# Query and key transposes taken before the high/low split, with ScalarE row sums and earlier weight splits

## The chip, the cores and the metric

The kernel runs on one core of one Trainium2 chip. The metric is the device time of one launch in microseconds (us); lower is better. Four engines compute: TensorE (PE in the profile, with its weight loads as PEld), VectorE (DVE), ScalarE (ACT) and GpSimd (POOL). SyncE (SP) issues the DMAs.

## The reference

One encoder layer on a sequence of 1024 tokens of width 1024, in float32:

```python
x = LN0(alpha*x + 0.5*SwiGLU_1(x))
u = x @ W_in                    # -> q | k | v | z | x_ssd | B | C | dt
q = rope(rms(q) * q_norm)       # 8 query heads of 64
k = rope(rms(k) * k_norm)       # 2 key/value heads of 64
a = softmax(q @ k.T / 8) @ v    # every 4 query heads share one key/value head
s = bidirectional chunked SSD scan of conv(x_ssd, B, C), gated by SiLU(z)
x = LN1(alpha*x + concat(a, s) @ W_out)
x = LN2(alpha*x + 0.5*SwiGLU_2(x))
x = LN3(alpha*x + sigmoid(x @ W_g + b_g) * (p @ W_p))
```

`rms` divides a head's 64 values by the root of their mean square. `rope` turns pairs of values by an angle that depends on the token.

## The kernel before

Matrix products run on a rounded float32 type (`F32R`). To keep the precision, most factors are split in two: the rounded value ("hi") and the rest ("lo", the plain value less hi). `mm3` (L116) forms a product from three matmuls for each block of 128: hi with lo, lo with hi, hi with hi. A split is one ScalarE copy (L108) and one VectorE subtraction (the helper `lo`, L87).

The part that matters here is `qkv_part` (L841). It comes between the last tiles of z (`z_part`) and the products that feed the convolution (`xbc_gemm`, L967).

- **q stage.** For each of 8 tiles of 128 tokens, `qq` (L832) multiplies the tile with the q weights: 24 matmuls of 512 columns into one buffer of the PSUM pool `sm`, which has four.
- **kv stage.** For each of the same 8 tiles, `kv` (L820) does it with the weights of k, v and dt: 24 matmuls of 272 columns into an `sm` buffer.
- **Behind each product**, `norm` (L862) squares the heads on ScalarE (L865), sums the squares on VectorE (L867), scales them (L868) and takes the power -0.5 on GpSimd (L870). `rope` (L873) refines that power (`newton`, L125), multiplies the values by it (L877, the last reader of the product's `sm` buffer) and turns them (L883 to L885) into the tile `qn`.
- **The split before the transpose.** `q_back` (L917) copies `qn` to the hi half of a tile `qs` on ScalarE (L920); the lo half is a VectorE subtraction, done one step later through the list `los`. So one head is 128 values wide, hi beside lo. `turn` transposes each of the 8 heads on TensorE (L926) into a buffer of the pool `big` (two buffers), and one ScalarE copy (L927) writes `Q`, with hi in 64 partitions and lo in the other 64. `kv_back` (L899) does the same for k: each of the two heads is written twice side by side, its hi half and its lo half are transposed apart (4 transposes, L909, into an `sm` buffer), and one copy (L910) writes `K`.
- **v** is split straight from the product (L895, L896), and dt is added to its bias (L892).

`step` (L933) sets the order: for tile t it issues the transposes of an earlier tile, then `norm` of t, then the outstanding `lo`, then `rope` of tile t-1. The transposes of a q tile stand behind the product three tiles later. What is left of k is put into `pend`, and `xbc_gemm` issues it between its halves.

The order on TensorE is the program's (`in_order`). The other engines' orders, and the buffers, are set by a planner that goes by its own estimates; `behind(engine)` makes what follows queue behind the last instruction written for that engine.

Weights come in by DMA from the SP queue into one of two `raw` buffers, and are split from there into a `blk` buffer of the pool `ring`, which has ten. In the q stage the eight blocks of q weights hold eight of them. `kv_weights` (L812) loads and splits the eight blocks for k, v and dt at tiles 6 and 7 of q, so six of them need a buffer that a q block leaves. `xbc_weights` (L961) loads and splits two blocks for each of the eight groups of convolution channels where the group's product is written.

Of the kernel before, what the change touches and what calls it, by code (L numbers as in the profile page):

```python
# [9 lines left out]
F32 = mybir.dt.float32  # L10
F32R = mybir.dt.float32r
BF16 = mybir.dt.bfloat16
AF = mybir.ActivationFunctionType
ALU = mybir.AluOpType
# [22 lines left out]
class Layer:  # L37
# [773 lines left out]

    def kv_weights(self, part):  # L812
        if part == 0:
            self.wkv = []
        for k in ((0,), (3, 6))[part]:
            n = min(3, KD - k)
            r = self.raw(self.I["wkv"][:, k * 272:(k + n) * 272], n * 272)
            self.wkv += [self.split(r[:, i * 272:(i + 1) * 272], 272) for i in range(n)]

# [21 lines left out]
    def qkv_part(self, c, xT):  # L841
        nc, tc, I = self.nc, self.tc, self.I
        Q, K, V = self.qkv
        tabs = c.enter_context(tc.tile_pool(name="tabs", bufs=1))
        wk = c.enter_context(tc.tile_pool(name="qwork", bufs=2))
        cs = tabs.tile([P, NT, HD], F32, name="cs")
        sn = tabs.tile([P, NT, HD], F32, name="sn")
# [14 lines left out]
        def norm(ps, nh):  # L862
            v = ps.rearrange("p (h d) -> p h d", d=HD)
            sq = wk.tile([P, nh, HD], F32, name="sq")
            nc.scalar.activation(out=sq, in_=v, func=AF.Square)  # L865
            ss = self.small.tile([P, 16], F32, name="ss")[:, :nh]
            nc.vector.reduce_sum(ss, sq, axis=AX.X)  # L867
            nc.vector.tensor_scalar(out=ss, in0=ss, scalar1=1.0 / HD, scalar2=RMS_EPS, op0=ALU.mult, op1=ALU.add)  # L868
            r = self.small.tile([P, 16], F32, name="qr")[:, :nh]
            nc.gpsimd.tensor_tensor(out=r, in0=ss, in1=self.mhalf[:, :nh], op=ALU.pow)  # L870
            return v, nh, sq, ss, r

        def rope(v, nh, m, ss, r, nm, t):  # L873

            self.newton(r, ss, nh)
            qn = wk.tile([P, nh, HD], F32, name="qn")
            nc.vector.tensor_tensor(out=qn, in0=v, in1=r.unsqueeze(2).broadcast_to([P, nh, HD]), op=ALU.mult)  # L877
            T1, T2 = (x[:, t] for x in T[nm])
            H2 = HD // 2
            for a in range(2):  # L880
                o = slice(a * H2, (a + 1) * H2)
                i = slice((1 - a) * H2, (2 - a) * H2)
                nc.vector.tensor_tensor(out=m[:, :, o], in0=qn[:, :, i], in1=T2[:, o].unsqueeze(1).broadcast_to([P, nh, H2]), op=ALU.mult)  # L883
            nc.vector.tensor_tensor(out=qn, in0=qn, in1=T1.unsqueeze(1).broadcast_to([P, nh, HD]), op=ALU.mult)
            nc.vector.tensor_tensor(out=qn, in0=qn, in1=m, op=ALU.add)  # L885
            return qn

# [11 lines left out]
        def kv_back(t, st):  # L899

            kn = rope(*st, "k", t).unsqueeze(2).broadcast_to([P, NKV, 2, HD])
            kd = wk.tile([P, NKV, 2, 2, HD], F32R, name="qs", bufs=4)
            nc.scalar.copy(out=kd[:, :, 0], in_=kn)

            def turn():
                pt = self.pss().rearrange("p (g j t) -> p g j t", g=NKV, j=2)
                for g in range(NKV):
                    for j in range(2):
                        nc.tensor.transpose(out=pt[:, g, j], in_=kd[:, g, j].rearrange("p a d -> p (a d)").bitcast(F32), identity=self.ident)  # L909
                nc.scalar.copy(out=K[:, :, :, t * P:(t + 1) * P], in_=pt)  # L910
            late.append(turn)
            return kd[:, :, 1], kn, kd[:, :, 0]

# [3 lines left out]
        def q_back(t, st):  # L917
            qs = wk.tile([P, NQ, 2, HD], F32R, name="qs", bufs=4)
            qn = rope(*st, "q", t)
            nc.scalar.copy(out=qs[:, :, 0], in_=qn)  # L920

            def turn():
                pt = self.psb().rearrange("p (h t) -> p h t", t=P)
                qv = qs.bitcast(F32)
                for hh in range(NQ):
                    nc.tensor.transpose(out=pt[:, hh], in_=qv[:, hh].rearrange("p a d -> p (a d)"), identity=self.ident)  # L926
                nc.scalar.copy(out=Q[:, :, t * P:(t + 1) * P], in_=pt)  # L927
            late.append(turn)
            return qs[:, :, 1], qn, qs[:, :, 0]

        backs, los = [], []

        def step(t, ps, front, back, keep=1):  # L933
# [5 lines left out]
            if los:  # L939
                self.lo(*los.pop())  # L940
            if backs:
                los.append(backs.pop()())
            if front:
                backs.append(lambda: back(t, st))

        tables("q", HD ** -0.5)
        for t in range(NT):
            ps = self.qq(t, xT)
            if t >= NT - 2:
                self.kv_weights(t - NT + 2)  # L950
            step(t, ps, q_front, q_back)
        for t in range(NT):
            ps = self.kv(t, xT)
            step(t, ps, kv_front, kv_back, 2)
            if t == 0:
                tables("k", 1.0)
        self.pend += [lambda: step(NT, None, None, None)] * 4
        self.x0 = self.xbc_gemm(0, xT, 1)
        assert not late and not backs and not los

    def xbc_weights(self, j):  # L961
        return [b.rearrange("p l (k c) -> p l k c", c=P) for b in self.wload(self.I["wx"][j])]

# [1056 lines left out]
```

## Time and profile before

| | |
|---|---|
| time, median of 3 runs | 1940.51 us (1940.17 to 1941.06) |
| profiled execution | 1940.12 us |
| its span, first to last instruction | 1938.3 us |
| PE busy | 1927.8 us (99%) |
| DVE busy | 1523.9 us (79%) |
| ACT busy | 881.6 us (45%) |
| POOL busy | 417.2 us (22%) |
| granted TensorE clock | 0.999 |

The span and all busy times are of the profiled execution; 1.8 us of its time lie outside the span. In rows of the profile, L12 is line 12 of the kernel, `out<-in` names the tiles written and read (buffer numbers left out), `x8` is a count, and `<-` in brackets names what ended an engine's idle time. Instructions of one engine overlap a little, so a start-to-start distance is the better measure of what one costs. In this profile the q stage's first product begins at about 696 us, the kv stage's at 744.35 us and the first convolution product at 772.90 us.

### The profile page before, as it was taken

The numbers are of one execution on the slowest core, as the hardware profiler recorded it, in microseconds if no ns is written. First come the engines' busy times: TensorE is split into PE (matmuls) and PEld (weight loads), VectorE is DVE, ScalarE is ACT, GpSimd is POOL, SyncE is SP. The second block draws the span as 40 slices with busy tenths as digits, with TensorE's granted clock in tenths as the row PEclk, the third lists the DMA queues.
The fourth block names the chain that finished last, engine by engine and source line by source line (L and its number), as shares of the span: only waits on it lengthen the run. The fifth ranks groups of instructions, "written<-read, shape, count | busy, mean of one in ns | idle before, by whom it ended". The sixth has DMA issues, their size and how long they took to land.

```text
span 1938.3 us, 25689 instructions
## 1 busy us (share of the span) xinstructions
PE 1927.8 (99%) x9146; PEld 1607.8 (83%) x9146; DVE 1523.9 (79%) x2362; ACT 881.6 (45%) x1510; POOL 417.2 (22%) x308
## 2 busy tenths in 40 slices
PE   9999999999999999999999999999999999999998
PEld 7888888888888889888888888888888888888886
DVE  8977777767678668758998888997787786877698
ACT  7433333334444224538897877633333333444311
POOL 0144544430001032001131001014444540001011
PEclk9999999999999999999999999999999999999999
DMA  8334544549866111241002663253544539976022
GB/s 315 127 130 153 194 181 147 195 163 389 280 220 210 63 43 48 86 123 67 6 1 85 219 215 122 93 176 138 190 175 168 183 122 359 331 263 223 28 78 97
DMA packets 147714, 310.34 MB, mean 160 GB/s; under 512 B 18129, under 2 KB 30801, under 8 KB 147585
## 3 DMA queue, kind: packets, MB, share of 16 engines
q1 hardware_dynamic: 147584, 308.69, 45.6%
q8 instruction: 72, 1.18, 0.2%
q14 instruction: 58, 0.47, 0.1%
HBM read 217.21 MB, written 91.42 MB: 159 GB/s over the span
## 4 chain that ended last, share of the span: by engine, by line
PE 99%; DVE 0%; DMA 0%; ACT 0%; DVEq 0%; issue 0%; SPq 0%
PE sm L122 56%; PE big L519 12%; PE sm L519 9%; PE big L122 6%; PE big L1189 3%; PE sm L1211 3%; PE sm L1226 2%; PE sm L1227 1%; PE sm L639 1%; PE sm L1407 1%; PE sm L1306 1%; PE sm L1317 1%; PE big L1722 0%; PE big L926 0%; PE big L224 0%; PE sm L224 0%
## 5 line engine op out<-in xcount | busy, mean ns | idle before, releaser
L122 PE MATMUL sm<-xh,blk 128*128 128x512 f32 x1424 | 439.8, 389 | 0.0
L122 PEld LDWEIGHTS sm<-xh,blk 128*128 128x128 f32 x1424 | 267.3, 188 | 55.4
L122 PE MATMUL sm<-xl,blk 128*128 128x512 f32 x736 | 283.8, 389 | 0.0
L122 PE MATMUL sm<-blk,xl 128*128 128x512 f32 (+2 forms) x704 | 208.1, 369 | 0.0
L108 ACT CAST blk<-raw 128x512 fp32r<-128x512 f32 (+1 forms) x168 | 101.1, 611 | 214.8 <-PE sm L122 133.2
L87 DVE TENSOR_TENSOR blk<-raw,blk 128x512 fp32r<-128x512 f32 (+1 forms) x168 | 142.5, 852 | 53.8 <-ACT blk L108 53.2
L108 ACT CAST blk<-s 128x512 fp32r<-128x512 f32 x172 | 105.7, 622 | 153.3 <-PE sm L122 125.7
L87 DVE TENSOR_TENSOR blk<-s,blk 128x512 fp32r<-128x512 f32 x176 | 142.3, 812 | 39.6 <-ACT blk L108 36.8
L178 POOL TENSOR_TENSOR ln_k<-ln_k,mhalf 128x1 f32<-128x1 f32 x32 | 37.7, 1183 | 578.4 <-DVE ln_k L177 562.2
L122 PEld LDWEIGHTS sm<-xl,blk 128*128 128x128 f32 x736 | 138.2, 188 | 28.7
L122 PE MATMUL sm<-blk,xh 128*128 128x512 f32 (+2 forms) x448 | 158.0, 373 | 0.0
L122 PEld LDWEIGHTS sm<-blk,xl 128*128 128x128 f32 x704 | 127.8, 188 | 20.6
L267 POOL TENSOR_TENSOR s<-raw 128x512 f32<-128x512 f32 x34 | 57.8, 1699 | 381.9 <-DVE blk L87 370.6
L519 PE MATMUL big<-xh 128*128 128x512 f32 x576 | 138.8, 390 | 0.0
L87 DVE TENSOR_TENSOR xh<-blk,xh 128x1024 fp32r<-128x1024 f32 x78 | 95.3, 1222 | 52.1 <-ACT xh L465 46.1
L465 ACT CAST xh<-blk 128x1024 fp32r<-128x1024 f32 x78 | 82.2, 1054 | 109.0 <-PE big L519 47.1
L465 ACT CAST xl<-blk 128x1024 fp32r<-128x1024 f32 x76 | 80.2, 1055 | 112.9 <-PE sm L519 43.1
L87 DVE TENSOR_TENSOR xl<-blk,xl 128x1024 fp32r<-128x1024 f32 x76 | 92.9, 1222 | 43.1 <-ACT xl L465 40.8
L519 PEld LDWEIGHTS big<-xh 128*128 128x128 f32 x576 | 107.8, 188 | 22.2
L519 PE MATMUL big<-xl 128*128 128x512 f32 x480 | 115.8, 390 | 0.0
L122 PE MATMUL sm<-xET2h,blk 128*128 128x512 f32 x352 | 108.4, 389 | 0.0
L122 PE MATMUL sm<-xET3h,blk 128*128 128x512 f32 x352 | 108.3, 389 | 0.0
(357 smaller groups left out, 4118.6 us busy)
## 6 DMA issues: line engine op xcount, KB each, us to landing
raw<-in_wi_dram SPq DMA_DIRECT2D x81, 512.0 KB
blk<-hS SPq DMA_DIRECT2D x154, 256.0 KB
hS<-h SPq DMA_DIRECT2D x88, 256.0 KB
wr<-in_wo_dram SPq DMA_DIRECT2D x44, 512.0 KB
blk<-wT SPq DMA_DIRECT2D x88, 256.0 KB
hS<-sg SPq DMA_DIRECT2D x66, 256.0 KB
wT<-wr SPq DMA_DIRECT2D x66, 256.0 KB
blk<-in_wo_dram SPq DMA_DIRECT2D x66, 256.0 KB
```

The lines of the kernel that those rows point to most:

```text
L87: (eng or self.nc.vector).tensor_tensor(out=out, in0=full, in1=hi.bitcast(F32), op=ALU.subtract)
L108: self.nc.scalar.copy(out=b[:, 0, :n], in_=src)
L122: self.nc.tensor.matmul(ps, lhsT=a, rhs=b, start=(i == 0), stop=(i == n - 1))
L178: nc.gpsimd.tensor_tensor(out=r, in0=v, in1=self.mhalf[:, :1], op=ALU.pow)
L267: lambda: G.tensor_tensor(out=s1, in0=a21, in1=a22, op=ALU.add),
L465: A.copy(out=b[:, :, 0], in_=r)
L519: nc.tensor.matmul(ps[q], lhsT=b[:, 0, x, cut], rhs=b[:, 1, y], start=j == i == 0, stop=j == NP - 1 and i == 2)
L639: nc.tensor.matmul(o, lhsT=pT[t // 4][k][:, i, c], rhs=we[n][k][:, j], start=k + i + j == 0, stop=k + i == 2)
L1189: nc.tensor.matmul(ps[:, n * 512:(n + 1) * 512], lhsT=Q[:, h, q0:q0 + P], rhs=K[:, h // 4, j, n * 512:(n + 1) * 512], start=j == 0, stop=j ...
L1211: nc.tensor.transpose(out=pt[:, k], in_=pr[:, kk * P:(kk + 1) * P], identity=self.ident)
L1226: nc.tensor.matmul(po, lhsT=vw, rhs=pth[k // 4][:, k % 4], start=k == 0, stop=False)
L1227: nc.tensor.matmul(po, lhsT=vw, rhs=ptl[k // 4][:, k % 4], start=False, stop=k == KD - 1)
```

## The change

Four things change in `qkv_part` and what it calls.

1. **Transposes of plain values.** For q, `turn` transposes two heads at a time from `qn` (4 transposes instead of 8). The split comes behind it: ScalarE copies each half of the partitions to its heads' hi place in `Q` (2 copies of 64 partitions), and VectorE subtracts into the other half (2 subtractions). The ScalarE copy into `qs` and the subtraction ahead of the transpose go. For k, the last addition of `rope` writes the head twice (`kn`), each head is transposed once (2 transposes instead of 4), and the split to `K` is one copy and one subtraction. `qn` and `kn` have four buffers.
2. **Sums of squares of q on ScalarE.** Eight activations of 64 columns with an accumulated sum replace one of 512 columns and VectorE's reduction. For k both stay.
3. **k-and-v weights** are split at tiles 2, 4 and 6 of q. Six blocks go to a pool of their own (`wkvp`), two to `ring`.
4. **The first two groups of convolution weights** (`self.wx`) are loaded and split behind kv tiles 3 and 5, in the order of ScalarE and VectorE, instead of where their products are written.

```diff
--- before.py
+++ after.py
@@ -809,13 +809,11 @@
         self.nc.sync.dma_start(out=t, in_=self.I[key].broadcast_to([P, n]))
         return t
 
-    def kv_weights(self, part):
-        if part == 0:
-            self.wkv = []
-        for k in ((0,), (3, 6))[part]:
-            n = min(3, KD - k)
-            r = self.raw(self.I["wkv"][:, k * 272:(k + n) * 272], n * 272)
-            self.wkv += [self.split(r[:, i * 272:(i + 1) * 272], 272) for i in range(n)]
+    def kv_weights(self, ks, pool):
+        r = self.raw(self.I["wkv"][:, ks[0] * 272:(ks[-1] + 1) * 272], len(ks) * 272)
+        for i, k in enumerate(ks):
+            b = pool.tile([P, 2, 272], F32R, name="wkv") if k < 6 else self.ring.tile([P, 2, 512], F32R, name="blk")
+            self.wkv.append(self.split_into(b, r[:, i * 272:(i + 1) * 272], 272))
 
     def kv(self, t, xT):
         ps = self.pss()
@@ -843,6 +841,7 @@
         Q, K, V = self.qkv
         tabs = c.enter_context(tc.tile_pool(name="tabs", bufs=1))
         wk = c.enter_context(tc.tile_pool(name="qwork", bufs=2))
+        kvp = c.enter_context(tc.tile_pool(name="wkvp", bufs=6))
         cs = tabs.tile([P, NT, HD], F32, name="cs")
         sn = tabs.tile([P, NT, HD], F32, name="sn")
         nc.sync.dma_start(out=cs, in_=I["cs"])
@@ -862,9 +861,13 @@
         def norm(ps, nh):
             v = ps.rearrange("p (h d) -> p h d", d=HD)
             sq = wk.tile([P, nh, HD], F32, name="sq")
-            nc.scalar.activation(out=sq, in_=v, func=AF.Square)
             ss = self.small.tile([P, 16], F32, name="ss")[:, :nh]
-            nc.vector.reduce_sum(ss, sq, axis=AX.X)
+            if nh == NQ:
+                for h in range(nh):
+                    nc.scalar.activation(out=sq[:, h], in_=v[:, h], func=AF.Square, accum_out=ss[:, h:h + 1])
+            else:
+                nc.scalar.activation(out=sq, in_=v, func=AF.Square)
+                nc.vector.reduce_sum(ss, sq, axis=AX.X)
             nc.vector.tensor_scalar(out=ss, in0=ss, scalar1=1.0 / HD, scalar2=RMS_EPS, op0=ALU.mult, op1=ALU.add)
             r = self.small.tile([P, 16], F32, name="qr")[:, :nh]
             nc.gpsimd.tensor_tensor(out=r, in0=ss, in1=self.mhalf[:, :nh], op=ALU.pow)
@@ -873,7 +876,7 @@
         def rope(v, nh, m, ss, r, nm, t):
 
             self.newton(r, ss, nh)
-            qn = wk.tile([P, nh, HD], F32, name="qn")
+            qn = wk.tile([P, nh, HD], F32, name="qn", bufs=4)
             nc.vector.tensor_tensor(out=qn, in0=v, in1=r.unsqueeze(2).broadcast_to([P, nh, HD]), op=ALU.mult)
             T1, T2 = (x[:, t] for x in T[nm])
             H2 = HD // 2
@@ -882,8 +885,13 @@
                 i = slice((1 - a) * H2, (2 - a) * H2)
                 nc.vector.tensor_tensor(out=m[:, :, o], in0=qn[:, :, i], in1=T2[:, o].unsqueeze(1).broadcast_to([P, nh, H2]), op=ALU.mult)
             nc.vector.tensor_tensor(out=qn, in0=qn, in1=T1.unsqueeze(1).broadcast_to([P, nh, HD]), op=ALU.mult)
-            nc.vector.tensor_tensor(out=qn, in0=qn, in1=m, op=ALU.add)
-            return qn
+            if nm == "q":
+                nc.vector.tensor_tensor(out=qn, in0=qn, in1=m, op=ALU.add)
+                return qn
+            kn = wk.tile([P, NKV, 2, HD], F32, name="kn", bufs=4)
+            a, b = (x.unsqueeze(2).broadcast_to([P, NKV, 2, HD]) for x in (qn, m))
+            nc.vector.tensor_tensor(out=kn, in0=a, in1=b, op=ALU.add)
+            return kn
 
         NK = NKV * HD
         late = []
@@ -898,35 +906,33 @@
 
         def kv_back(t, st):
 
-            kn = rope(*st, "k", t).unsqueeze(2).broadcast_to([P, NKV, 2, HD])
-            kd = wk.tile([P, NKV, 2, 2, HD], F32R, name="qs", bufs=4)
-            nc.scalar.copy(out=kd[:, :, 0], in_=kn)
+            kn = rope(*st, "k", t)
 
             def turn():
-                pt = self.pss().rearrange("p (g j t) -> p g j t", g=NKV, j=2)
+                pt = self.pss()[:, :NKV * P].rearrange("p (g t) -> p g t", g=NKV)
                 for g in range(NKV):
-                    for j in range(2):
-                        nc.tensor.transpose(out=pt[:, g, j], in_=kd[:, g, j].rearrange("p a d -> p (a d)").bitcast(F32), identity=self.ident)
-                nc.scalar.copy(out=K[:, :, :, t * P:(t + 1) * P], in_=pt)
+                    nc.tensor.transpose(out=pt[:, g], in_=kn[:, g].rearrange("p a d -> p (a d)"), identity=self.ident)
+                hi, lo = (K[:, :, j, t * P:(t + 1) * P] for j in range(2))
+                nc.scalar.copy(out=hi, in_=pt)
+                self.lo(lo, pt, hi)
             late.append(turn)
-            return kd[:, :, 1], kn, kd[:, :, 0]
 
         def q_front(t, ps):
             return norm(ps, NQ)
 
         def q_back(t, st):
-            qs = wk.tile([P, NQ, 2, HD], F32R, name="qs", bufs=4)
             qn = rope(*st, "q", t)
-            nc.scalar.copy(out=qs[:, :, 0], in_=qn)
 
             def turn():
-                pt = self.psb().rearrange("p (h t) -> p h t", t=P)
-                qv = qs.bitcast(F32)
-                for hh in range(NQ):
-                    nc.tensor.transpose(out=pt[:, hh], in_=qv[:, hh].rearrange("p a d -> p (a d)"), identity=self.ident)
-                nc.scalar.copy(out=Q[:, :, t * P:(t + 1) * P], in_=pt)
+                pt = self.psb()[:, :512].rearrange("p (h t) -> p h t", t=P)
+                for hp in range(NQ // 2):
+                    nc.tensor.transpose(out=pt[:, hp], in_=qn[:, 2 * hp:2 * hp + 2].rearrange("p h d -> p (h d)"), identity=self.ident)
+                both = [(slice(e * HD, (e + 1) * HD), slice((1 - e) * HD, (2 - e) * HD), Q[:, e::2, t * P:(t + 1) * P]) for e in range(2)]
+                for mine, other, q in both:
+                    nc.scalar.copy(out=q[mine], in_=pt[mine])
+                for mine, other, q in both:
+                    self.lo(q[other], pt[mine], q[mine])
             late.append(turn)
-            return qs[:, :, 1], qn, qs[:, :, 0]
 
         backs, los = [], []
 
@@ -938,28 +944,35 @@
             st = front(t, ps) if front else None
             if los:
                 self.lo(*los.pop())
-            if backs:
-                los.append(backs.pop()())
+            if backs and (todo := backs.pop()()):
+                los.append(todo)
             if front:
                 backs.append(lambda: back(t, st))
 
         tables("q", HD ** -0.5)
+        self.wx = []
+        self.wkv, kv_ks = [], {2: (0, 1, 2), 4: (3, 4, 5), 6: (6, 7)}
         for t in range(NT):
             ps = self.qq(t, xT)
-            if t >= NT - 2:
-                self.kv_weights(t - NT + 2)
+            if t in kv_ks:
+                self.kv_weights(kv_ks[t], kvp)
             step(t, ps, q_front, q_back)
         for t in range(NT):
             ps = self.kv(t, xT)
             step(t, ps, kv_front, kv_back, 2)
             if t == 0:
                 tables("k", 1.0)
+            if t in (3, 5):
+                r = self.raw(self.I["wx"][t // 2 - 1])
+                with self.behind(mybir.EngineType.Activation), self.behind(mybir.EngineType.DVE):
+                    self.wx.append([self.split(r[:, i * 512:(i + 1) * 512]) for i in range(2)])
         self.pend += [lambda: step(NT, None, None, None)] * 4
         self.x0 = self.xbc_gemm(0, xT, 1)
         assert not late and not backs and not los
 
     def xbc_weights(self, j):
-        return [b.rearrange("p l (k c) -> p l k c", c=P) for b in self.wload(self.I["wx"][j])]
+        blocks = self.wx[j] if j < len(self.wx) else self.wload(self.I["wx"][j])
+        return [b.rearrange("p l (k c) -> p l k c", c=P) for b in blocks]
 
     def xbc_half(self, w, xT, h, ps):
         self.mm3(ps, [((w[k // 4][:, 0, k % 4], w[k // 4][:, 1, k % 4]), tuple(x[:, k % 4] for x in xT[h][k // 4])) for k in range(KD)])
```

## The prediction

> **What bounds the kernel now.** I read the page first: its busy times and its chain of what ended last.
>
> ```profile
> span 1938.3 us, 25689 instructions
> PE 1927.8 (99%) x9146; PEld 1607.8 (83%) x9146; DVE 1523.9 (79%) x2362; ACT 881.6 (45%) x1510; POOL 417.2 (22%) x308
> PE 99%; DVE 0%; DMA 0%; ACT 0%; DVEq 0%; issue 0%; SPq 0%
> ```
>
> TensorE is busy for 99% of the span and carries 99% of the chain. No other engine ends a wait worth naming. So what leaves TensorE shortens the kernel, what is added elsewhere is free while it stays hidden, and the way to lose is a new TensorE wait. Next comes the chain in order of time through the q and kv stages (start, us, what):
>
> ```profile
> 737.39 0.87 PE big L926 x8
> 738.26 5.46 PE sm L122 x24
> 743.72 0.87 PE big L926 x8
> 744.60 6.08 PE sm L122 x48
> ...
> 762.33 0.44 PE sm L909 x4
> 762.77 3.01 PE sm L122 x24
> 765.78 0.44 PE sm L909 x4
> 766.22 3.04 PE sm L122 x24
> ...
> 772.71 0.44 PE sm L909 x4
> 773.14 5.47 PE big L122 x24
> 778.62 0.87 PE sm L909 x8
> ```
>
> Each piece starts where the one before it ends: TensorE never waits here. Eight transposes take 0.87 us and four take 0.44, so one costs 0.109 us, with no fixed part (0.87 - 2 x 0.44 = -0.01). A q product takes 5.46, a kv product 3.01 to 3.04. The counts come from the views of the two lines:
>
> ```profile
> L926 PE MATMUL big<-ident,qs x64: 270/273/273, 718.2 to 759.1; 128*128 128x128 f32 x64
> L909 PE MATMUL sm<-ident,qs x32: 270/272/273, 762.2 to 785.6; 128*128 128x128 f32 x32
> ```
>
> The 0.27 us is one transpose from end to end; they overlap, so the chain's 0.109 is the price.
>
> **The change, part by part.**
>
> *Transposes.* q goes from 64 to 32, k from 32 to 16: 48 x 0.109 = **5.23 us off TensorE**. Shape and type (128x128 f32) stay, so the price should too. [...]
>
> *Squares and copies on ScalarE.* Prices from the groups by form, and one row of ScalarE's timeline:
>
> ```profile
> L1138 ACT ACTIVATE cd<-sm 128x64 f32<-128x64 f32 x2 | 0.4, 216 | 0.0
> L1481 ACT ACTIVATION_READ_ACCUMULATOR ysq<-y 128x1 f32 x16 | 3.0, 187 | 0.0
> L1233 ACT COPY a_raw<-sm 64x512 f32<-64x512 f32 x16 | 9.3, 582 | 5.0 <-PE sm L1227 4.7
> 1123.55 2.01 ACT L1300 ACTIVATE state<-state,cd 128x64 f32<-128x64 f32 x8
> ```
>
> Eight 64-column activations with a read of the sum each: no less than 2.0 us (eight such activations without the read), no more than 8 x (0.216 + 0.187) = 3.2. I take 3.2, since each read has a row of its own. What goes, in one tile:
>
> ```profile
> 724.81 0.60 ACT L865 ACTIVATE sq<-sm 128x512 f32<-128x512 f32 x1 [2.26 <-PE sm L122]
> 725.62 1.02 ACT L927 CAST Q<-big 128x1024 fp32r<-128x1024 f32 x1 [0.21 <-PE big L926]
> 727.50 0.62 ACT L920 CAST qs<-qn 128x512 fp32r<-128x512 f32 x1 [0.86 <-DVE qn L885]
> ```
>
> These 2.24 us become 3.2 + 2 x 0.58 = 4.4 in a q tile of 5.46 + 0.44 = 5.90. ScalarE's share rises to 75%, still hidden.
>
> *VectorE in the q stage.* Prices from its groups and its timeline:
>
> ```profile
> L87 DVE TENSOR_TENSOR xh<-big,xl 128x512 fp32r<-128x512 f32 x16 | 11.0, 686 | 10.8 <-ACT xl L228 10.7
> 710.85 0.69 DVE L87 TENSOR_TENSOR qs<-qn,qs 128x512 fp32r<-128x512 f32 x1 [0.69 <-ACT qs L920]
> 725.46 0.68 DVE L867 TENSOR_REDUCE ss<-sq 128x8 f32<-128x512 f32 x1
> 739.68 0.90 DVE L87 TENSOR_TENSOR blk<-raw,blk 128x272 fp32r<-128x272 f32 x2
> ```
>
> A tile loses the reduction (0.68) and the subtraction from `qn` (0.69), and gains two subtractions from PSUM. No row shows one of 64 partitions; between nothing and the 128-partition 0.686 I take 0.686, as ScalarE's 64-partition copy (0.582) is no cheaper for having half the lanes. Net 0.00. The k-and-v splits add 8 x 0.45 = 3.6 us to the q stage; before, most of them fell on its end and the start of the kv stage. The windows show what is free (length, then busy PE, PEld, DVE, ACT, POOL):
>
> ```profile
> 724.55:730.88 6.33, 6.33 (x33) 5.33 (x32) 5.22 (x14) 2.24 (x3) 2.06 (x1) 1.00 0.00 0
> ```
>
> VectorE has 5.22 of 5.90 us to do per tile, and 3.6 us of splits over the five tiles 2 to 6, or 0.72 a tile: 5.9 of 5.9. It may lag, and the lag is covered. Tile 0's values are finished at 711.54 (the row at 710.85), its transposes come only at 718.37 (718.2 to 759.1 above, by instruction), so some 6.8 us of lag cost nothing. POOL's power operations and their number stay.
>
> *DMAs and SP.* The three loads for k, v and dt and the eight for the convolution keep number and size. The first two of the latter move up:
>
> ```profile
> 740.14 0.33 SPq L94 DMA_DIRECT2D raw<-in_wkv_dram  x1
> 742.08 39.07 SPq L94 DMA_DIRECT2D raw<-in_wx_dram  x7
> ```
>
> In SP's queue they pass only the third k-and-v load, which now waits for the `raw` buffer that tile 2's splits free, some 25 us earlier than now. Behind it stand only these same loads. Nothing.
>
> *The kv stage.* Here I expect the trouble. k's subtraction stays at 128x256, but the addition doubles in size; convolution splits come in between. VectorE's timeline:
>
> ```profile
> 757.65 0.29 DVE L885 TENSOR_TENSOR qn<-qn,sq 128x128 f32<-128x128 f32 x1
> 758.48 0.42 DVE L87 TENSOR_TENSOR qs<-qn,qs 128x256 fp32r<-128x256 f32 x1
> 761.39 0.29 DVE L877 TENSOR_TENSOR qn<-sm,qr 128x128 f32<-128x128 f32 x1
> 764.88 0.29 DVE L877 TENSOR_TENSOR qn<-sm,qr 128x128 f32<-128x128 f32 x1
> 767.02 0.29 DVE L877 TENSOR_TENSOR qn<-sm,qr 128x128 f32<-128x128 f32 x1
> 771.04 0.69 DVE L87 TENSOR_TENSOR blk<-raw,blk 128x512 fp32r<-128x512 f32 x1
> ```
>
> The three L877 rows are tiles 2, 3 and 4; each frees its product's `sm` buffer. At 766.22 tile 6's product starts. It, tile 5's product, the transposes of 765.78 and tile 4's product (read until 767.31) fill all four buffers, so tile 3's must be free: it was at 765.17. **The margin is 1.05 us.** After the change that product comes 3 x 0.44 + 2 x 0.22 = 1.76 us sooner, counted from the stage's start, so VectorE would be 0.71 us late if it ran as now. What it must do before tile 3's L877: gone are one 272-column and two 512-column weight splits (0.45 + 1.38), two q subtractions (1.38), one reduction (0.68) and three k subtractions (1.26), 5.2; new are eight subtractions behind the transposes of q tiles 4 to 7 (5.5), one behind those of k's tile 0 (0.42), the two splits behind tile 3 (1.4) and three larger additions (3 x 0.13), 7.7. So 2.5 more. The windows of VectorE alone give its idle time:
>
> ```profile
> 744.60:755.60 11.00, 9.52 (x30) 1.00 0.33 109
> 755.60:762.50 6.90, 6.30 (x36) 1.00 0.00 0
> ```
>
> That is 1.48 + 0.60 = 2.1 us idle, for 2.5 more work. Part of the idle time and of the delay was ScalarE's order:
>
> ```profile
> 761.11 0.41 ACT L903 CAST qs<-qn 128x256 fp32r<-128x256 f32 x1 [0.73 <-DVE qn L885]
> 761.42 0.27 ACT L865 ACTIVATE sq<-sm 128x128 f32<-128x128 f32 x1
> ```
>
> The second row is tile 3's square. Its product ended at 758.5 (744.60, plus 6.08 for tiles 0 and 1, two groups of q transposes and tiles 2 and 3: 2 x 0.87 + 2 x 3.02), yet it queued behind a cast that waited for VectorE. That cast goes. So TensorE's wait lies between 0 (the earlier square gives the margin back) and 0.71 + 2.5 = 3.2 us (idle time stays idle). I take **0.7**, nearer the lower end: the idle time and the earlier square absorb the added work, the lost margin remains. Four of k's subtractions move past the stage's end, which helps the tiles after that.
>
> *After the stage.* Convolution weights are ready sooner and VectorE holds fewer splits between 771 and 785 us. TensorE did not wait there before (the chain at 773.14), so nothing is gained.
>
> **Sum.** Profiled execution 1940.12 us (span 1938.3): -5.23 + 0.7 = 1935.6. The median of runs, 1940.51, lies 0.4 above it: **1936.0 us**, 0.23% less.
>
> **The rivals.**
>
> *A, VectorE holds up the kv stage.* Idle time does not get used, since an engine's order is fixed ahead and a waiting instruction holds up the rest. Price: 3.2 us at tile 6's product, and up to 1.4 more for the two splits behind tile 5, which stand before tile 5's L877; gain 5.2 - 3.2 = 2.0 or 5.2 - 4.6 = 0.6, so 1938.5 to 1939.9. For it: the 1.05-us margin. Against it: the cast leaves ScalarE's order. It decides from a wait of 1.3 us, where the gain falls under 0.2%.
>
> *B, slower: VectorE and ScalarE run in series in the q stage.* If each tile's subtractions stand early in VectorE's order, they wait for the Q copies, which wait for the squares: 3.2 + 1.16 = 4.4 us without VectorE, then its 5.2 us: 9.6 a tile against 5.9. Over the five tiles with transposes, 18.5 us late, less the 6.8 us of slack: 11.7 of wait, less 5.2, some 6.5 slower: 1947. The result is slower by 0.2% once waits pass 5.2 + 3.9 = 9.1 us. For it: the square that queued behind a cast shows such blocking. Against it: q tiles are three products ahead of their transposes, and VectorE has other work to be ordered first. [...]
>
> *C, the transposes are worth less.* If a transpose cost half when fewer stand together, 48 would give 2.6 us: 1937.9. The 0.44 for four against 0.87 for eight speaks against it. [...]
>
> **How the numbers follow.** 0.2% of the time is 3.9 us, about what a measurement of this kernel can tell from no change: faster means under 1936.6. The forecast (waits up to 1.3 us) has 0.61 and by itself reaches from 1934.9 to 1936.6. A has 0.29, all within 0.2%; B 0.07; C 0.03, also within 0.2%. That makes 0.61 faster, 0.32 same, 0.07 slower. The range starts at no wait with the runs' scatter of 0.4 us (1934.9) and goes up through the middle of A, to 1939.0; B and A's tail are left out.
>
> **What would show it.** Half the transposes of q and k, groups of four in q taking 0.44 us and of two in k 0.22. Pieces of the chain still end to end in the q stage. One gap on TensorE before a kv product from the fifth on, under 1 us, with tile 3's or 4's L877 as releaser. ScalarE near 75% in the q stage, its squares group 2 to 3.2 us. The prediction is wrong if TensorE shows waits in q tiles (B), more than 1.3 us of them in the kv stage (A), or transposes under 0.1 us apiece (C).

## The result, and the profile after

The changed kernel takes 1945.22 us (median of 12 runs, 1943.98 to 1946.15) against 1940.53 for the kernel before: a ratio of 1.0024, with a 95% interval of 1.0016 to 1.0032. It is slower by 4.7 us where 4.5 less was forecast, and lies above the range. One of the 12 runs of the kernel before took 2280.39 us and is left out of the ratio. The page of the profiled execution, its span, busy times and chain:

```profile
span 1943.0 us, 25728 instructions
PE 1926.4 (99%) x9098; PEld 1604.4 (83%) x9098; DVE 1530.4 (79%) x2362; ACT 882.9 (45%) x1622; POOL 415.3 (21%) x308
PE 95%; DVE 3%; POOL 1%; DMA 0%; issue 0%; ACT 0%; DVEq 0%; ACTq 0%
```

The 48 transposes are gone (9146 matmuls became 9098), yet the chain now runs through VectorE and GpSimd for 4% of the span. Where that is, two lines of each kernel tell: the first transposes of q, and the first attention products (by instruction: least, median and most ns, then first and last start). First the kernel before (its transposes stand in the prediction), then after:

```profile
L1189 PE MATMUL big<-K,Q x256: 387/392/481, 874.6 to 1048.2; 128*128 128x512 f32 x128
```

```profile
L929 PE MATMUL big<-ident,qn x32: 270/272/301, 718.9 to 756.8; 128*128 128x128 f32 x32
L1202 PE MATMUL big<-K,Q x256: 387/392/481, 878.2 to 1051.7; 128*128 128x512 f32 x128
```

I call the stretch between the two the stage. It took 156.41 us before (718.20 to 874.61, the timeline's finer starts) and 159.29 after (718.88 to 878.17). Without the transposes it should have taken 156.41 - 5.23 = 151.18, so TensorE **lost 8.11 us** there. The other differences of the two spans: 0.68 ahead of the stage (below), 0.17 in and just behind attention, and 0.99 in the SSD stage. 2.88 + 0.68 + 0.17 + 0.99 = 4.72, and the spans differ by 4.7.

TensorE's timeline of the changed kernel shows the loss; in brackets stand the idle time ahead of the instruction and what ended it. Before, there was none:

```profile
756.47 0.63 PE L929 MATMUL big<-ident,qn 128*128 128x128 f32 x4 [0.38 <-DVE qn L889]
763.40 0.44 PE L914 MATMUL sm<-ident,kn 128*128 128x128 f32 x2 [3.30 <-DVE qn L880]
765.12 0.59 PE L122 MATMUL sm<-wkv,xl 128*128 128x272 f32 x1 [1.28 <-DVE K L87]
...
776.42 0.44 PE L914 MATMUL sm<-ident,kn 128*128 128x128 f32 x2 [0.19 <-DVE K L87]
...
788.96 0.41 PE L914 MATMUL sm<-ident,kn 128*128 128x128 f32 x2 [0.49 <-DVE kn L893]
```

The five waits come to 5.6 us. Each costs some 0.16 us more than its length, 0.8 in all, because matmuls overlap: in this timeline a 272-column one lasts 0.29 us and the next starts 0.13 us after it. The worst stands ahead of the transposes of k's tile 0: they need an `sm` buffer, the four are held by the products of kv tiles 1 to 4, and tile 1's is freed by its L880 (L877 before) only at 763.05 + 0.29. The rest is the clock, which the windows of TensorE give (length, busy, granted clock, DMA share, GB/s):

```profile
763.00:764.00 1.00, 0.44 (x2) 1.00 0.00 0
764.00:765.00 1.00, 0.00 (x0) 0.89 0.00 0
765.00:766.00 1.00, 0.88 (x4) 0.50 0.00 0
766.00:767.00 1.00, 1.00 (x6) 0.50 0.00 0
767.00:768.00 1.00, 1.00 (x6) 0.50 0.00 0
768.00:769.00 1.00, 1.00 (x9) 0.91 0.00 0
```

From 764.8 to 768.2 TensorE runs at half clock. The fall comes 1.4 us after the long wait has ended, inside the next one (763.84 to 765.12), and lasts well beyond it; 0.11 + 3 x 0.50 + 0.09 = 1.70 us of full-speed time are lost, some 0.2 of them while TensorE waits anyway.

Why was L880 of tile 1 late? Its product had ended by 749.04, when the next group of transposes started. VectorE's timeline, tile 1's steps and what stood between them:

```profile
756.94 1.39 DVE L87 TENSOR_TENSOR Q<-big,Q 64x512 fp32r<-64x512 f32 x2
...
758.62 0.28 DVE L870 TENSOR_REDUCE ss<-sq 128x2 f32<-128x128 f32 x1
...
759.32 1.39 DVE L87 TENSOR_TENSOR Q<-big,Q 64x512 fp32r<-64x512 f32 x2
...
760.95 0.16 DVE L871 TENSOR_SCALAR ss<-ss 128x2 f32<-128x2 f32 x1
...
763.05 0.29 DVE L880 TENSOR_TENSOR qn<-sm,qr 128x128 f32<-128x128 f32 x1
```

And ScalarE's, the squares of kv tiles 0, 1 and 2:

```profile
749.13 0.28 ACT L869 ACTIVATE sq<-sm 128x128 f32<-128x128 f32 x1 [3.23 <-DVE qn L889]
756.42 0.28 ACT L869 ACTIVATE sq<-sm 128x128 f32<-128x128 f32 x1 [2.12 <-DVE qn L889]
761.76 0.28 ACT L869 ACTIVATE sq<-sm 128x128 f32<-128x128 f32 x1 [3.44 <-DVE kn L893]
```

Two things delay the chain square, sum, mean, power, scaling. The square waits for VectorE, since the tile `sq` has two buffers and `rope` of the tile two earlier still uses one of them (the releasers L889 and L893 are its last reads). Then its small steps queue behind the subtractions of q's late tiles: 1.39 us for two halves, twice within tile 1's chain.

The delay begins in the q stage, where TensorE waits for nothing yet. The chain that ended last leaves TensorE at 713.6 us, at the squares of q tile 2, and comes back only at 765.12. From q tile 6's mean (L871) to tile 7's it reads (start, us, what):

```profile
741.37 0.18 DVE ss L871
...
741.62 2.02 POOL qr L873
...
744.47 0.70 DVE qn L880
...
745.99 0.69 DVE Q L87
746.69 0.70 DVE Q L87
...
747.41 0.69 DVE qn L887
748.10 0.08 DVE ss L871
...
765.12 4.65 PE sm L122 x24
```

One round from mean to mean holds a tile's power on GpSimd, its scaling on VectorE, and Q's subtractions of an older tile, which stand ahead of the next mean. From tile 3's mean (723.04) to tile 7's (748.02) a round takes 6.25 us, where TensorE needs 5.92 for a tile (718.88 to 742.57). So VectorE and GpSimd fall behind TensorE, and the lag is handed on to k's norms.

### The profile page after: what moved, and what is told of

Its sections match the earlier page's. It is cut to its first block, busy times and chain, and to the rows that moved or that the text cites. A ratio compares the mean times of both kernels' runs of the same rounds, so it can differ in the third digit from the quotient of the medians.

```text
span 1943.0 us, 25728 instructions
## 1 busy us (share of the span) xinstructions
PE 1926.4 (99%) x9098; PEld 1604.4 (83%) x9098; DVE 1530.4 (79%) x2362; ACT 882.9 (45%) x1622; POOL 415.3 (21%) x308
## 4 chain that ended last, share of the span: by engine, by line
PE 95%; DVE 3%; POOL 1%; DMA 0%; issue 0%; ACT 0%; DVEq 0%; ACTq 0%
PE sm L122 54%; PE big L519 12%; PE sm L519 9%; PE big L122 6%; PE big L1202 3%; PE sm L1224 3%; PE sm L1239 2%; PE sm L1240 1%; PE sm L639 1%; POOL qr L873 1%; DVE Q L87 1%; PE sm L1420 1%; PE sm L1319 1%; PE sm L1330 1%; PE big L224 0%
## 5 line engine op out<-in xcount | busy, mean ns | idle before, releaser
L122 PE MATMUL sm<-blk,xl 128*128 128x512 f32 (+2 forms) x608 | 189.7, 381 | 0.0
L122 PE MATMUL sm<-blk,xh 128*128 128x512 f32 (+2 forms) x400 | 144.1, 383 | 0.0
L122 PEld LDWEIGHTS sm<-blk,xl 128*128 128x128 f32 x608 | 112.7, 188 | 20.8
```

The costliest lines, as they stand in the source:

```text
L122: self.nc.tensor.matmul(ps, lhsT=a, rhs=b, start=(i == 0), stop=(i == n - 1))
```

## The experiments

The theories. **1**: VectorE is the trouble, as an amount of work in the kv stage, or (sharper) as a queue in which small steps stand behind long ones. **2**: the loop of two `sq` buffers. **3**: too few `sm` buffers. **4**: the early splits of convolution weights. Each edit makes the planner write the orders of all engines but TensorE anew, so a run never differs in one instruction alone, and no run holds those orders fixed. Results:

| run | median us | ratio to before, 95% interval | stage us | lost in it |
|---|---|---|---|---|
| changed kernel | 1945.22 | 1.0024 (1.0016 to 1.0032) | 159.29 | 8.11 |
| turns_only | 1944.33 | 1.0021 (1.0012 to 1.0030) | 159.95 | 8.77 |
| no_wx | 1944.24 | 1.0019 (1.0010 to 1.0028) | 159.01 | 7.83 |
| sq_only | 1940.15 | 0.9999 (0.9990 to 1.0007) | 156.41 | none |
| lo_act | 1940.18 | 0.9999 (0.9990 to 1.0008) | 154.51 | 3.33 |
| sqk | 1942.54 | 1.0011 (1.0003 to 1.0020) | 157.47 | 6.29 |
| kbig | 1947.92 | 1.0037 (1.0024 to 1.0051) | 162.99 | 11.81 |
| kact | 1942.04 | 1.0005 (0.9996 to 1.0014) | 155.31 | 4.13 |
| kact_pool | 1940.22 | 1.0001 (0.9992 to 1.0010) | 155.15 | 3.97 |
| kact_gss | 1937.64 | 0.9986 (0.9977 to 0.9995) | 152.87 | 1.69 |
| act_all | 1942.94 | 1.0015 (1.0006 to 1.0024) | 156.85 | 5.67 |
| act_all_gss | 1943.10 | 1.0014 (1.0005 to 1.0023) | 157.79 | 6.61 |
| gss_only | 1941.73 | 1.0008 (0.9999 to 1.0017) | 155.91 | 4.73 |

("Lost" is the stage of the profiled run less 151.18; for sq_only, which keeps all transposes, less 156.41. The profiled run was the fastest of its kernel in lo_act, kact and act_all (1939.24, 1939.37 and 1941.41 us), so a typical run of these may lose more.)

**Parts alone.** turns_only is the kernel before with part 1 (its hunks in `rope`, `kv_back`, `q_back` and `step`), sq_only the kernel before with part 2 (the hunk in `norm`), no_wx the changed kernel without these lines:

```
-            if t in (3, 5):
-                r = self.raw(self.I["wx"][t // 2 - 1])
-                ...
-                    self.wx.append([self.split(...) for i in range(2)])
```

> The kernel before with the first part of the change alone: q and k transposed plain and split behind it; squares, k-and-v weights and convolution weights as before. TensorE work falls by 48 x 0.109 = 5.2 us, as in the changed kernel. Theory 1 (the subtractions of q tiles 5 to 7, six of 0.69 us, now fall on VectorE in the kv stage and delay the k norms, so that an sm buffer of PSUM comes free late): the wait remains, 3 to 9 us of lost TensorE time between 742 and 790 us, since here the k-and-v weight splits fall there too; 1939 to 1944. Rival 2 (ScalarE's squares wait for the two sq buffers): the same wait, with the sq wait of ScalarE in front of it. Rival 4 (the early splits of convolution weights in the kv stage are to blame): no wait over 1 us; 1935.3 to 1936.5.

> The kernel before with the second part alone: ScalarE sums q's squares in eight small activations, the transposes, splits and weights are as before. VectorE loses 0.68 us a q tile that was hidden, TensorE's work is the same, no wait expected: 1940.0 to 1941.0 by every theory. Of the 1.0 us that every kernel with part 1 lost in the SSD stage (first to last state product 33.98 us before, 34.88 to 35.33 in five others): if it belongs to what part 1 moves in memory, this kernel shows 33.9 to 34.1; if any other order of the stages ahead brings it, 34.8 or more and about 1941.3.

> The changed kernel, but the first two blocks of convolution weights are loaded and split where the kernel before did it, not in the kv stage. Theory 1: in the changed kernel the first of these splits ran on VectorE at 766.85, after the 3.30-us wait (760.1 to 763.4), so that wait and the half clock behind it stay; at most the later short waits (0.35 and 0.73 us) go: 1943.5 to 1945.5. Rival 4 (the early splits are to blame): the wait goes, 1938 to 1940.

Part 1 alone brings a loss as large (8.77) and two halvings of the clock, just above the 1944 expected at most, so the other parts are not needed for it. The way there differs in part: the chain that ended last passes through a k-and-v split that waits for its load (2.68 us from 740.56), and part 3 moves that split away. Part 2 alone changes nothing; part 3 alone, and parts 2 to 4 without part 1, were not run. Without the early splits the wait ahead of k's first transposes and the half clock go, which theory 1 had not expected, but other waits take their place (1.78 and 1.31 us ahead of q transposes, 1.14 ahead of a product) and 7.83 us stay lost: theory 4 falls.

**Less VectorE work behind q's transposes** (lo_act; the lo halves of q tiles 5 to 7 are plain values, as the expectation says).

```
                 for mine, other, q in both:
-                    self.lo(q[other], pt[mine], q[mine])
+                    if t > 4:
+                        nc.scalar.copy(out=q[other], in_=pt[mine])
+                    else:
+                        self.lo(q[other], pt[mine], q[mine])
```

> The changed kernel, but the lo halves of Q for tiles 5 to 7 are written by ScalarE copies of the plain value instead of VectorE's subtractions (their values are then not the remainders). VectorE loses 6 x 0.69 = 4.2 us in the kv stage, ScalarE gains 6 x 0.58 = 3.5. Theory 1: tile 1's L880 comes 3 us or more sooner (before 760.5), the 3.30-us wait ahead of k0's transposes falls under 0.7, the clock does not halve behind it, and 6 to 7 of the 8.1 lost us come back: 1938 to 1940. Rival 2 (the sq loop): ScalarE's square of kv tile 1 still waits for q7's L889 until about 755, so a wait of 1.5 us or more remains; 1940 to 1942. Rival 3 (too few sm buffers): the wait moves little; 1942 to 1945.

TensorE's waits in the stage:

```profile
760.09 0.39 PE L122 MATMUL sm<-wkv,xl 128*128 128x272 f32 x1 [1.12 <-DVE K L87]
764.50 0.39 PE L122 MATMUL sm<-wkv,xl 128*128 128x272 f32 x1 [0.92 <-DVE K L87]
771.52 0.44 PE L914 MATMUL sm<-ident,kn 128*128 128x128 f32 x2 [0.51 <-DVE K L87]
```

The 3.30 us ahead of k's first transposes and the half clock are gone, and tile 1's L880 comes at 758.01. 4.8 of the 8.1 us come back where 6 to 7 were expected, the half clock's 1.7 among them, for 4.2 us taken off VectorE. The median, 1940.18, lies just above theory 1's range and within theory 2's, but no wait reaches the 1.5 us of theory 2. Theory 1 holds, in one of its two forms.

**The buffers.** sqk gives k's squares two buffers of their own (and `kn` three for four); kbig puts k's transposes into `big`.

```
-            sq = wk.tile([P, nh, HD], F32, name="sq")
+            sq = wk.tile([P, nh, HD], F32, name="sq" if nh == NQ else "sqk")
```

```
-                pt = self.pss()[:, :NKV * P].rearrange(...)
+                pt = self.psb()[:, :NKV * P].rearrange(...)
```

> The changed kernel, but k's squares have two buffers of their own (sqk) beside q's two, so the square of kv tile 0 or 1 no longer waits until rope of q tile 6 or 7 has read its buffer; kn has three buffers instead of four to make room. Rival 2 (the sq loop): ScalarE's square of tile 1 runs at about 749.5 instead of 756.4, its L880 before 759.5, no wait over 0.7 us ahead of k0's transposes, no half clock: 1938 to 1940. Theory 1 (VectorE's amount of work): the norms wait in VectorE's queue just as long, L880 of tile 1 comes at most 1 us sooner, wait of 2.3 us or more: 1943 to 1945.

> The changed kernel, but k's transposes go into buffers of the pool big, so that the four sm buffers serve products alone. Rival 3 (too few sm buffers): no wait over 0.7 us is left in the kv stage, 1938 to 1940. Theories 1 and 2: tile 1's buffer is still free only at about 763; k0's transposes no longer need it, but tile 5's product does, which stands right behind them at about 760.3: a wait of 2.5 to 2.9 us there instead of 3.30 and 1.28. Lost TensorE time 4 to 6 us instead of 8.1, depending on whether the clock halves after so short a wait: 1941 to 1943.5.

In sqk the square of kv tile 1 and its L880 (759.28) run when theory 2 said, but TensorE's largest wait has only moved to the transposes of q's last tile (ScalarE's timeline, then TensorE's):

```profile
749.56 0.28 ACT L869 ACTIVATE sqk<-sm 128x128 f32<-128x128 f32 x1 [0.73 <-DVE dt L900]
```

```profile
758.16 0.63 PE L929 MATMUL big<-ident,qn 128*128 128x128 f32 x4 [2.06 <-DVE qn L889]
```

So the loop is real but worth 1.8 us of the stage, and that is nearly all the half clock, which did not come: the waits fall only from 5.6 to 5.0. What k gains in VectorE's queue, q's last tile loses. The 1942.54 us lie between the ranges of the two theories. kbig is worse than anything else, which none of the theories had said: k's subtractions then hold one of only two `big` buffers, and a convolution product (0.89 us at 775.23) and k's own next transposes (1.69 at 782.89) wait for them. Theory 3 falls, and `big` is no place for k.

**Work moved off VectorE.** In kact ScalarE sums k's squares and scales k; in kact_pool GpSimd also multiplies k's tables (L858); in act_all ScalarE scales q too; in the runs with gss the mean (L871) is made on GpSimd. The lines are shortened, with several runs' edits in one and notes behind them:

```
-                nc.scalar.activation(out=sq, in_=v, func=AF.Square)
-                nc.vector.reduce_sum(ss, sq, axis=AX.X)
+                nc.scalar.activation(out=sq[:, h], in_=v[:, h], func=AF.Square, accum_out=ss[:, h:h + 1])   # per head; sq is k's qn tile
-            nc.vector.tensor_tensor(out=qn, in0=v, in1=r..., op=ALU.mult)                                    # kact: k; act_all: q too
+            nc.scalar.activation(out=qn[:, h], in_=v[:, h], func=AF.Identity, scale=r[:, h:h + 1])           # per head
-            nc.vector.tensor_scalar(out=ss, in0=ss, scalar1=1.0 / HD, scalar2=RMS_EPS, ...)                  # gss
+            nc.gpsimd.tensor_scalar(out=ss, in0=ss, scalar1=1.0 / HD, scalar2=RMS_EPS, ...)
```

> The changed kernel with less VectorE work for each kv tile: ScalarE sums k's squares (two activations of 64 columns) and multiplies k by its power (two more), so VectorE loses the reduction (0.28) and L880 (0.29); the squares go into the tile that k is scaled into, which takes k's squares out of the loop of two sq buffers. Theory 1 (VectorE bounds the kv stage; ScalarE's loop adds to it): about 1.4 us less VectorE work ahead of tile 1's release and the 1.8 us that the own sq buffers were worth; the lost 8.1 us become 3 to 5, no half clock: 1940 to 1942. Rival 3 (PSUM buffers): the buffers are freed after the power operation by whichever engine, nothing changes: 1944 to 1946.

> As the run before it, and GpSimd multiplies the two tables of k's rope (VectorE 2 x 0.68 us at 754.84 and 756.24 in the changed kernel). Theory 1: another 1.4 us off VectorE at the critical place, 1.0 to 1.4 us faster than the run before it: 1938.8 to 1941. If GpSimd's slower products stand ahead of k's power operations in its queue, they hold those up instead and the time is that of the run before it or worse.

> The kernel of the run kact, and the step that turns a sum of squares into a mean (L871 of the changed kernel, 0.17 us, which waited in VectorE's queue behind Q's subtractions of 1.39 us) goes to GpSimd, just ahead of the power. Theory 1 in its sharper form (not VectorE's hours but its queue: small steps of the chain stand behind long ones): tile 1's power starts 1 to 3 us sooner, the waits of 1.12, 1.32 and 0.98 us seen in kact shrink to under 2 together: 1937.5 to 1940. If only VectorE's total work counts, 10 small operations of 0.17 us bring under 1 us: 1941 to 1942. If GpSimd's added step (0.7 to 1 us) lengthens every chain, 1942 or more.

> The kernel of the run kact, and q's scaling too (L880, 0.69 us of VectorE for each of eight tiles) goes to ScalarE, eight activations of 64 columns. ScalarE in the q stage rises from 2.9 to about 3.8 us of 5.6. Theory 1: tiles 6 and 7 of q leave VectorE 1.4 us sooner, the wait ahead of q7's transposes (1.12 us in kact) goes and the later two shrink: 1938.5 to 1941. If the waits in the kv stage come from k's chain alone, 1941 to 1942.5.

> Both of the two runs before it together: k's sums, k's and q's scaling on ScalarE, the mean on GpSimd. Theory 1: the kv stage loses under 1.5 us in all, so that the 5.2 us of saved transposes are kept but for that: 1936 to 1938.5, faster than the kernel before by 1.8 to 4 us. If the waits have another cause, no better than the best of the two: 1939 or more.

> The changed kernel with one edit: the step from the sum of squares to the mean (L871, 0.17 us on VectorE, 16 times) runs on GpSimd ahead of the power; k's sums and scaling stay on VectorE, the loop of two sq buffers stays. VectorE loses only some 10 x 0.07 to 0.17 us ahead of tile 1's release. If VectorE's total work sets the waits: 1 us or less faster, 1944 to 1946. If it is the place of this small step in VectorE's queue (in the changed kernel tile 1's sum was ready at 758.8 and its mean came at 760.95, behind the 1.39 us of a Q subtraction; q7's stood behind two longer ones), tile 1's release comes about 2 us sooner, the 3.30-us wait falls under 1.5 us and the clock does not halve: 1940 to 1942.5. Neither 1.5 us nor more than that tells both apart alone: 1942.5 to 1944 leaves both with a share.

gss_only is the changed kernel with the last edit alone. Moving sixteen steps of 0.17 us gives 3.4 us of the stage back, the half clock's 1.7 among them. First VectorE's rows of q tile 7 in the changed kernel (its mean, and the last reading of its `sq`), then GpSimd's, VectorE's and TensorE's in gss_only:

```profile
748.02 0.17 DVE L871 TENSOR_SCALAR ss<-ss 128x8 f32<-128x8 f32 x1
...
755.64 0.68 DVE L889 TENSOR_TENSOR qn<-qn,sq 128x512 f32<-128x512 f32 x1
```

```profile
745.46 0.20 POOL L871 TENSOR_SCALAR ss<-ss 128x8 f32<-128x8 f32 x1 [4.02 <-ACT sq L867]
...
756.16 0.19 POOL L871 TENSOR_SCALAR ss<-ss 128x2 f32<-128x2 f32 x1 [7.50 <-DVE ss L870]
```

```profile
752.78 0.69 DVE L889 TENSOR_TENSOR qn<-qn,sq 128x512 f32<-128x512 f32 x1
...
755.79 0.28 DVE L870 TENSOR_REDUCE ss<-sq 128x2 f32<-128x128 f32 x1
...
760.08 0.29 DVE L880 TENSOR_TENSOR qn<-sm,qr 128x128 f32<-128x128 f32 x1
```

```profile
760.43 0.44 PE L914 MATMUL sm<-ident,kn 128*128 128x128 f32 x2 [0.51 <-DVE qn L880]
```

kv tile 1's release comes 3.0 us sooner, and the 3.30-us wait is 0.51. The expectation had put this down mainly to tile 1's own mean, but its chain from sum to scaling is hardly shorter (4.29 us against 4.43): the mean follows its sum after 0.4 us instead of 2.3, and a later small step (L131 at 759.30) waits behind Q's subtractions instead. What comes sooner is the sum, by 2.8 us, because q tile 7 is done sooner. Its mean runs as soon as ScalarE has the sums (745.46), no longer behind Q's subtractions (748.02); so its last reading of `sq` comes 2.9 us sooner, and tile 1's square at 753.87 instead of 756.42. This much shows in more runs than one: counted from the stage's first transposes, tile 7's power begins at 29.3 to 29.4 us in the changed kernel, lo_act, sqk, kbig, kact and kact_pool, and at 27.3 in gss_only and kact_gss. The order alone can move it too: no_wx, with the mean on VectorE, has 28.1. What the new order did behind that, no run separates.

kact and kact_pool came out about as theory 1 said (4.13 and 3.97 us lost, no half clock). kact_gss beats both kernels: 0.14% faster than before, one wait of 1.40 us in the stage. act_all takes q's scaling off VectorE as well and is slower than kact_gss. One window of each from the end of q's products on, over the same TensorE work of 16.8 us (length, busy PE, PEld, DVE, ACT, POOL), kact_gss first:

```profile
742.80:760.80 18.00, 16.84 (x137) 16.60 (x135) 16.84 (x55) 10.60 (x51) 5.42 (x10) 1.00 0.01 2
```

```profile
742.40:763.30 20.90, 16.75 (x133) 16.27 (x132) 16.69 (x60) 13.25 (x68) 5.60 (x5) 1.00 0.00 1
```

The same TensorE work takes 18.0 us with VectorE 94% busy, and 20.9 with VectorE 80% busy. So VectorE's occupancy does not set the time here. In act_all_gss, which has nearly the same waits, one sees what does (ScalarE's timeline, then VectorE's):

```profile
752.36 1.75 ACT L880 ACTIVATE qn<-sm,qr 128x64 f32<-128x64 f32 x8 [1.71 <-DVE rs_t L131]
```

```profile
754.14 0.76 DVE L886 TENSOR_TENSOR sq<-qn,T 128x256 f32<-128x256 f32 x2 [1.40 <-ACT qn L880]
```

ScalarE needs 1.75 us for what VectorE did in 0.69, and VectorE's queue stands still for it. My theory in its first form, the amount of work, fails here and in gss_only (1944 to 1946 expected by it, 1941.73 measured). The queue form agrees with gss_only and kact_gss, and no run contradicts it, but it is argued from orders that the planner chose. It did not foresee kbig, nor act_all and act_all_gss: 1938.5 to 1941 and 1936 to 1938.5 were expected by theory 1, 1942.94 and 1943.10 measured, since I had not counted the longer chain through ScalarE.

## Why the prediction was wrong

**Right.** The transposes are worth what was said: half of them are gone and a group of four takes 0.44 us (here in the chain of sqk, which has the same q stage), so C is out. In the q stage TensorE waits for nothing, so B is out at its price of 9.6 us a tile, though a round of VectorE and GpSimd there did take longer than TensorE's tile (6.25 against 5.92):

```profile
719.05 0.44 PE big L929 x4
```

```profile
718.90:724.80 5.90, 5.90 (x30) 4.89 (x29) 4.13 (x8) 2.90 (x18) 1.51 (x1) 1.00 0.00 0
```

A subtraction of 64 partitions takes 0.69 us (1.39 for two), as taken.

**Off without harm.** ScalarE's share in the q stage is 2.90 of 5.90, not 75%: eight squares with their sums take 1.76 us, under both ends of my 2.0 to 3.2. The k-and-v splits were not put into the q stage but ahead of it (661.9 to 668.2).

**The step that failed** is the kv stage: "I take **0.7**, nearer the lower end: the idle time and the earlier square absorb the added work". It measured 8.1, beyond the upper end of 3.2, and makes 7.4 of the 9.2 us between forecast and result.
- The place was wrong. I tested one buffer, tile 3's at tile 6's product. The first shortage came at the transposes of k's tile 0, with tile 1's buffer. Before, that buffer was free at 759.83, and these transposes began at 762.17 (VectorE's row, then TensorE's):

```profile
759.54 0.29 DVE L877 TENSOR_TENSOR qn<-sm,qr 128x128 f32<-128x128 f32 x1
```

```profile
762.17 0.60 PE L909 MATMUL sm<-ident,qs 128*128 128x128 f32 x4
```

- The margin of 2.3 us there was lost twice over. Counted from the stage's first transposes, after the change the buffer came free 2.8 us later and TensorE was ready 2.8 us sooner. My 1.76 us for the second counted the kv stage alone and left out the transposes saved in the q stage.
- "It may lag, and the lag is covered" failed with it. VectorE was busy for only 4.13 of 5.90 us in the window above, yet fell behind, because it stood idle for the power (0.8 to 1.75 us a tile) and had Q's subtractions ahead of the next mean. The slack of the q tiles hid this from TensorE; the margin of k's norms was too small for that.
- The earlier square did not come. I had put its delay down to the cast in ScalarE's order; the cast went, but the squares of tiles 0 to 2 waited 2.1 to 3.4 us for VectorE's last read of `sq`, and tile 3's ran at 764.82 instead of 761.42.
- Work was added up as a sum against idle time. What counted was which instructions stood ahead of the small steps. Rival A named that (an order fixed ahead, a waiting instruction that holds up the rest) and was priced too low, at 4.6 at most: it took one or two waits, where the late chain gave five, and no loss of clock.
- The half clock, 1.70 us of full-speed time, was in no case of mine.

**Not foreseen and not settled: 0.99 us in the SSD stage.** VectorE waits there for a buffer whose transfer to memory is under way, first before, then after:

```profile
1100.15 0.69 DVE L1397 TENSOR_TENSOR y<-xb,dsk 128x512 f32<-128x512 f32 x1 [1.02 <-DMA yd<-y]
```

```profile
1104.88 0.69 DVE L1410 TENSOR_TENSOR y<-xb,dsk 128x512 f32<-128x512 f32 x1 [1.95 <-DMA yd<-y]
```

That stage, from the products of its first chunk (L1407, then L1420) to those of its last, took 34.0 us in the kernel before and in sq_only, 34.9 to 35.3 in eleven profiles with part 1, and 34.0 in a twelfth, kact's, whose profiled run is the fastest of its eleven. So it goes with part 1 mostly but not always, and no run here says why. The 0.68 us ahead of the stage arise within the first 29 us, in code that the change leaves alone: TensorE's first L639 products start at 6.77 us instead of 6.29, and anywhere from 5.74 to 6.77 in these profiles. I take it for scatter; with one profile of each kernel this is not shown.

## What to carry to other kernels

When a change shortens TensorE's stage, write down for each PSUM buffer which chain frees it, and follow that chain through every engine's queue: moving steps of 0.17 us out from behind subtractions of 1.39 gave back 3.4 of the 8.1 us lost here. Where several engines pass work round (mean, power, scaling, next mean), measure the round and not each engine's busy share. To relieve a full engine, move the small steps of the chain that others wait for, not the largest operations; a long operation moved to an engine that is slower at it (q's scaling: 1.75 us on ScalarE, 0.69 on VectorE) adds its time to the chain and leaves the queue standing. A buffer shared by two uses (`sq` for the squares and for `rope`: ScalarE stood idle for 2.1 to 3.4 us ahead of k's first three squares) is a wait between two tiles that no list of instructions shows.

## What the hardware showed

**The clock.** Each halving lost the same 1.70 us of full-speed time, 3.4 us at half: here once, twice in turns_only, once in kbig and act_all_gss. It does not follow from the length of the wait: 2.02 us brought one in turns_only, and the second one there came inside a wait of 1.09 us, with 0.44 us of work between it and one of 0.92, while 2.06 in sqk and 2.74 in act_all brought none, and act_all_gss with 2.68 and nearly the same order did have one. What sets it off, no run here shows.

**VectorE beside GpSimd.** In kact_pool some of VectorE's operations took longer while GpSimd's table products ran (1.29 us at 753.82, 1.26 at 755.75; on VectorE, in the changed kernel, 0.68 each):

```profile
754.02 1.65 DVE L891 TENSOR_TENSOR qn<-qn,T 128x512 f32<-128x512 f32 x1
...
755.77 0.69 DVE L87 TENSOR_TENSOR Q<-big,Q 64x512 fp32r<-64x512 f32 x1
756.49 1.07 DVE L893 TENSOR_TENSOR qn<-qn,sq 128x512 f32<-128x512 f32 x1
```

L891 and L893 take 0.68 to 0.71 us elsewhere in that profile and read two SBUF tiles; the subtraction between them reads one from PSUM and kept its 0.69. These are three rows of one profile, so whether that difference is the reason is not shown.
